# Low parts of the expert weights on VectorE, high parts a step ahead of them, X transposed beside the down products, loop over middle tiles behind the last tile

## The chip, the core and the metric

The kernel runs on one core of one Trainium2 chip. The metric is the device time of one execution in microseconds (us), as the median of several runs. The engines are named as the profile names them: PE is the matrix engine and PEld its loading of weights, DVE the vector engine, ACT the scalar engine, POOL or Pool is GpSimd, and SP is the engine whose queue issues most transfers. PEq, DVEq and so on stand for the sequencer of an engine.

## The reference

One decoder block over 1024 tokens of 1024 numbers, in float32. Two token mixers, a gated MLP over chunks and a windowed attention, come first, and neither is touched by the change. Behind them stands the mixture of experts, in which each token goes to two of 16 experts:

```python
def hierarchical_moe(h, rg_w, rg_b, re_w, re_b, w_gate, w_up, w_down):
    ...
    out = jnp.zeros_like(t)
    for e in range(N_EXPERTS):
        hid = jax.nn.silu(t @ w_gate[e]) * (t @ w_up[e])
        out = out + combine[:, e:e + 1] * (hid @ w_down[e])
    return out.reshape(B, S, D)
...
h = h + hierarchical_moe(hn, ...)
return rms_norm(h, final_norm_g)
```

## The kernel before

The projections, the mixers and the routing take the first 640 us or so. The routing writes each token's row into a queue in memory for each of its experts (`xs_d`). The expert stage then goes through the experts e = 0 to 15, one after the other, the last fourteen in an order by their number of tokens.

**Weights as granules.** The weights of an expert are 12 granules of 128 x 1024 numbers: eight of gate and up, in two transfers of 256 KB each, and four of down, in one of 512 KB. The transfers are issued in SP's queue and land in nine raw buffers. PE multiplies in a 32-bit format of fewer digits (`fp32r`), so each granule is split in two. The high part is a copy on ACT (line 292 with the scale of the norm for gate and up, line 297 for down). The low part is raw times scale minus high: on DVE for gate and up (line 295), and on Pool for the four granules named in `POOL_LO` (line 301), except for the last expert, whose four are on DVE. A matrix product is then three matmuls (lines 193 to 195): high x high, high x low, low x high. A raw buffer is free for its next load when the low part is done, and the split tile when PE has read it.

**One expert.** `expert_tile` computes a tile of 128 tokens. The gate and up products fill two PSUM banks, f = 0 and f = 1, in steps ("k", 0) to ("k", 3), then f = 0 to its end, then f = 1. `hidden(f)` is a silu on ACT (line 1361) and a product on DVE (line 1362). `hidden_T(f)` transposes the result on PE (line 1368) and splits it into `hT` (lines 170 and 171). Between hidden(0) and hidden_T(0) PE has only two steps, gate_up(1, 4) and gate_up(1, 5). Then come four down products (line 1406), with hidden_T(1) behind the first. The result is scaled into `yt`, one half on ACT (line 1423) and one on DVE (line 1424), and added to the rows of `h_d` by an indirect transfer that Pool issues (line 1429).

**Work ahead.** While the main tile of expert e runs, `ahead(step)` places the work for expert e + 1 between its steps: loads, splits of granules 3 to 11 as listed in `AHEAD` (`AHEAD_0` and `AHEAD_1` for e = 0 and 1), and the transposes of its tokens (`transpose_x`, line 1318). `split` issues the high part, the low part, and the load that takes the raw buffer next. All engines run their instructions in the order in which this code writes them, so an instruction that waits holds up all behind it on its engine.

**Last tiles.** In front of its main tile an expert with more than 128 tokens has a last tile (`more_tiles`). For a remainder of up to 64 it is a `half_tile` (names end in `h`: 2h, 4h, 6h, 8h, 10h in this data), else a full one (12l, 15l). With it the first two steps of the main tile are done, and granules 0 to 2 of the next expert are split: `fill(0)` and `fill(1)`. An expert of up to 128 tokens (the odd ones, and 14) does the two fills alone. Between the branch (line 1573) and the last tile stands a loop over middle tiles (lines 1574 and 1575), for experts with more than 256 tokens, which this data has none of: it is skipped.

The functions that the diff touches, and what calls them, with the line numbers of the profile:

Of the kernel before, what the change touches and what calls it, by code (L numbers as in the profile page):

```python
# [19 lines left out]
P = 128  # L20
# [28 lines left out]
FIRST = 3  # L49
AHEAD = {("k", 1): (3, 4), ("k", 2): (5,), ("f1", 5): (6, 7), ("f1", 7): (8,), ("y", 0): (9, 10), ("y", 1): (11,)}  # L50

AHEAD_0 = {("f1", 7): (3, 4), ("y", 0): (5, 6, 7), ("y", 1): (8, 9, 10, 11)}
AHEAD_1 = {("f1", 5): (3, 4, 5), ("f1", 7): (6,), ("y", 0): (7, 8, 9), ("y", 1): (10, 11)}
ORDER_AT = {("f1", 5), ("y", 2)}
# [6 lines left out]
BESIDE = {("k", 1), ("k", 2), ("k", 3), ("f1", 5), ("f1", 7), ("y", 0), ("y", 1)}  # L61

POOL_LO = (8, 9, 10, 11)

# [15 lines left out]
def kernel(  # L80
# [160 lines left out]
    class Granules:  # L241
# [41 lines left out]

        def fill(self, g, pool_lo=(), later=None):

            w, k = self.split_tiles[g], g % 12
            raw, hi, low = self.raw[g], w[:, 0, :], w[:, 1, :]
            if k < KT:  # L290
                f = g2T[:, k : k + 1]
                nc.scalar.activation(hi, raw, AF.Copy, scale=f)  # L292

                def lo():
                    nc.vector.scalar_tensor_tensor(low, raw, f, hi, ALU.mult, ALU.subtract)  # L295
            else:
                nc.scalar.activation(hi, raw, AF.Copy)  # L297
                eng = nc.gpsimd if k in pool_lo else nc.vector

                def lo():  # L300
                    eng.tensor_tensor(low, raw, hi, ALU.subtract)  # L301
            if later is None:
                lo()
            else:
                later.append(lo)

        def split(self, g, *args, **kw):

            while len(self.split_tiles) <= g:
                self.take(len(self.split_tiles))  # L310
            self.fill(g, *args, **kw)
            for more in LOAD_AFTER.get(g, (g + 9,)):
                self.load(more)

    granules = Granules()
    early = []
    lows = []
    region = ExitStack()
# [74 lines left out]
    with ExitStack() as dctx:  # L393
# [266 lines left out]
        def half(hf, xh, vln, first):  # L660
# [252 lines left out]
            for nh in range(2):  # L913
# [5 lines left out]
                for i in range(HT):  # L919
# [17 lines left out]
                    if last and i == HT - 1:  # L937
                        granules.split(7, later=lows)
                    routed = {i: i for i in range(HT)} if hf == 1 else {1: 0, 3: 2}
# [405 lines left out]
    def expert_tile(  # L1345
# [77 lines left out]
        nc.scalar.activation(yt[:, 0:512], ys[0], AF.Copy, scale=cw)  # L1423
        nc.vector.tensor_scalar(yt[:, 512:D], ys[1], cw, None, ALU.mult)
        if dup is not None:
# [115 lines left out]

    def hint_more(e, n):

        tc.mark_branch_hint_location(f"more{e}", hint=n > P, engines=[mybir.EngineType.PE])

    def more_tiles(e, n, xlast, mlast, fill, first):
# [25 lines left out]

        with tc.If(n > P, label=f"more{e}") as more:
            with tc.If(n > 2 * P):
                with tc.For_i(1, (n - 1) // P, 1) as j:
                    startm = nc.s_assert_within(
                        j * P + first_row(e), 0, NE * CAP - P,
                        skip_runtime_bounds_check_because="1 <= j < (n - 1) // P <= 7",
                    )
                    xm, mm = transpose_x(  # L1580
                        load_x(xs_d[bass.ds(startm, P), :], f"{e}m", "yt"), f"{e}m", xT=xT
                    )
                    expert_tile(xm, mm, e, None, f"{e}m", **banks)
            last_tile(f"{e}")
        with more.Else():
# [8 lines left out]
    xT, meta = transpose_x(xearly[0], "0", 2, xs_d[0:P, D:XW])  # L1594
    lows[0]()
    place_tables(slice(0, 2), ebase)
    xnext = first_rows(1)
    n, *lasts = last_rows(0)
    hint_more(0, n)
    for g in range(9, 15):  # L1600
        granules.split(g, POOL_LO)

    nc.scalar.activation(one, one, AF.Silu)
    ordering = order_experts()
    for e in range(NE - 1):
# [18 lines left out]
        def ahead(step):  # L1624
            if e == 0 and step in ORDER_AT:
                next(ordering)
            if step == ("k", 0):
                got["n"] = last_rows(e + 1)
            if step == ("f1", 5) and e + 2 < NE:
                hint_more(e + 1, got["n"][0])  # L1630
            if step == ("f1", 7):
                got["x"] = transpose_x(xnext, f"{e + 1}")
            for j in (AHEAD_0, AHEAD_1, AHEAD)[min(e, 2)].get(step, ()):
                if 12 * (e + 1) + j < 12 * NE:
                    granules.split(12 * (e + 1) + j, POOL_LO if e + 2 < NE else ())
            if step == ("y", 0) and e + 2 < NE:
                got["next"] = first_rows(e + 2)
# [231 lines left out]
```

## Time and profile before

| | |
|---|---|
| median of 3 runs | 1130.58 us (1128.57 to 1130.84) |
| the profiled execution | 1130.55 us, its span 1128.8 us |
| busy share of the span | PE 92%, DVE 64%, ACT 53%, POOL 25% |
| mean granted clock of PE | 0.965 |

The span runs from the first to the last instruction; 1.75 us lie around it. The busy shares are means over the whole span, the expert stage alone is what the change touches. Matmuls overlap, so their durations sum to more than the time they take. A row with "<-" at its end names what released the instruction from its wait.

### The profile page before, as it was taken

The page shows a single profiled execution, that of the slowest core. Times are in us where ns is not written, and L with a number is a line of the kernel's source. Part 1 is how long each engine was busy: PE and PEld are TensorE (multiplying, and loading weights), DVE is VectorE, ACT ScalarE, POOL GpSimd, SP SyncE. Part 2 cuts the span into 40 slices and gives each one's busy share as a digit, 9 for nine tenths or more (in the row PEclk, how much of TensorE's full clock was granted, in tenths as well). Part 3 has the DMA queues.
Part 4 walks back from the last instruction along what each step waited for, and adds up shares of the span by engine and source line. Part 5 has one row for each costly group of instructions (what it writes and reads, how often), then busy time and mean ns, then how long its engine had stood idle before and what let it go on. Part 6 is the DMA issues. An engine that isn't in the chain of part 4 may idle for free. (4 is left out here: it accounts for less than half of the span.)

```text
span 1128.8 us, 15722 instructions
## 1 busy us (share of the span) xinstructions
PE 1036.0 (92%) x4775; PEld 833.4 (74%) x4775; DVE 726.0 (64%) x1592; ACT 598.6 (53%) x1000; POOL 280.3 (25%) x196
## 2 busy tenths in 40 slices
PE   7999899999999999999999777899898989898973
PEld 6778788788888888877888655677676767686762
DVE  6852567664468546774465889676776666657754
ACT  4543456543456445553354355575756666647451
POOL 4001000000012000000000424554646464626433
PEclk9999899999999999999999888999999989999996
DMA  7433545653247223226473549798979897968763
GB/s 240 131 94 117 182 153 166 187 159 131 75 154 242 91 77 91 57 75 187 131 261 128 197 149 270 236 288 270 308 243 312 249 319 222 311 220 283 232 235 136
DMA packets 125502, 214.72 MB, mean 190 GB/s; under 512 B 11563, under 2 KB 58731, under 8 KB 125360
## 3 DMA queue, kind: packets, MB, share of 16 engines
q1 hardware_dynamic: 112016, 176.58, 48.3%
q0 software_dynamic: 7200, 21.20, 7.0%
q10 hardware_dynamic: 6144, 15.27, 3.7%
q8 instruction: 62, 1.02, 0.4%
q14 instruction: 80, 0.66, 0.2%
HBM read 185.46 MB, written 37.63 MB: 198 GB/s over the span
## 5 line engine op out<-in xcount | busy, mean ns | idle before, releaser
L295 DVE SCALAR_TENSOR_TENSOR w_e<-raw_e,g2T,w_e 128x1024 fp32r<-128x1024 f32 x127 | 193.3, 1572 | 12.4 <-ACT w_e L292 10.1
L301 POOL TENSOR_TENSOR w_e<-raw_e,w_e 128x1024 fp32r<-128x1024 f32 x59 | 152.0, 2609 | 55.7 <-ACT w_e L297 55.4
L292 ACT ACTIVATE w_e<-raw_e,g2T 128x1024 fp32r<-128x1024 f32 x127 | 138.2, 1143 | 15.7 <-DMA raw_e<-in_expert_w_up_dram 4.6
L1071 POOL COPY row<-ids 128x1 int32<-128x1 int32 x8 | 4.2, 523 | 439.5 <-DVE w_e L295 227.8
L193 PE MATMUL ps_gu<-w_e,xT 128*128 128x512 f32 x256 | 105.8, 413 | 6.8 <-ACT w_e L297 4.1
L195 PE MATMUL ps_gu<-w_e,xT 128*128 128x512 f32 x256 | 103.4, 404 | 0.0
L194 PE MATMUL ps_gu<-w_e,xT 128*128 128x512 f32 x256 | 102.8, 402 | 0.0
L1406 PE MATMUL ps_y<-w_e,hT 128*128 128x512 f32 x384 | 98.6, 406 | 0.8 <-DVE hT L171 0.8
L1406 PEld LDWEIGHTS ps_y<-w_e,hT 128*128 128x128 f32 x384 | 70.8, 192 | 16.4 <-DVE hT L171 1.4
L297 ACT ACTIVATE w_e<-raw_e 128x1024 fp32r<-128x1024 f32 x63 | 63.0, 1052 | 1.5 <-DMA raw_e<-in_expert_w_down_dram 1.4
L193 PEld LDWEIGHTS ps_gu<-w_e,xT 128*128 128x128 f32 x256 | 49.4, 193 | 18.9 <-issue 8.7
L195 PEld LDWEIGHTS ps_gu<-w_e,xT 128*128 128x128 f32 x256 | 49.6, 194 | 11.8
L194 PEld LDWEIGHTS ps_gu<-w_e,xT 128*128 128x128 f32 x256 | 49.6, 194 | 10.2
L195 PE MATMUL ps_o<-w_wo,ms 128*128 128x512 f32 x128 | 51.3, 402 | 0.0
L194 PE MATMUL ps_o<-w_wo,ms 128*128 128x512 f32 x128 | 51.2, 400 | 0.0
L193 PE MATMUL ps_o<-w_wo,ms 128*128 128x512 f32 x128 | 51.1, 400 | 0.0
L193 PE MATMUL ps_ga<-xh,w_ga 128*128 128x512 f32 x128 | 50.7, 396 | 0.0
L194 PE MATMUL ps_ga<-xh,w_ga 128*128 128x512 f32 x128 | 50.6, 396 | 0.0
L195 PE MATMUL ps_ga<-xh,w_ga 128*128 128x512 f32 x128 | 50.6, 396 | 0.0
L559 PE MATMUL ps_gv<-w_gv,xh 128*128 128x512 f32 x192 | 46.9, 397 | 4.0 <-ACT xh L170 2.6
L194 PE MATMUL ps_gb<-xh,w_gb 128*128 128x512 f32 x128 | 50.5, 395 | 0.0
L195 PE MATMUL ps_gb<-xh,w_gb 128*128 128x512 f32 x128 | 50.5, 395 | 0.0
(554 smaller groups left out, 2494.1 us busy)
## 6 DMA issues: line engine op xcount, KB each, us to landing
raw_e<-in_expert_w_gate_dram SPq DMA_DIRECT2D x127, 256.0 KB
raw_e<-in_expert_w_up_dram SPq DMA_DIRECT2D x127, 256.0 KB
raw_e<-in_expert_w_down_dram SPq DMA_DIRECT2D x63, 512.0 KB
xs_d<-zero ACTq DMA_DIRECT2D x16, 516.0 KB
raw_ga<-in_w_in_dram SPq DMA_DIRECT2D x16, 512.0 KB
raw_gb<-in_w_in_dram SPq DMA_DIRECT2D x16, 512.0 KB
raw_wo<-in_w_out_dram SPq DMA_DIRECT2D x16, 512.0 KB
xt<-xs_d SPq DMA_DIRECT2D x15, 516.0 KB
```

Source lines behind the costliest of these rows:

```text
L193: nc.tensor.matmul(acc, lhi, rhi, start=start, stop=False)
L194: nc.tensor.matmul(acc, lhi, rlo, start=False, stop=False)
L195: return nc.tensor.matmul(acc, llo, rhi, start=False, stop=stop)
L292: nc.scalar.activation(hi, raw, AF.Copy, scale=f)
L295: nc.vector.scalar_tensor_tensor(low, raw, f, hi, ALU.mult, ALU.subtract)
L297: nc.scalar.activation(hi, raw, AF.Copy)
L301: eng.tensor_tensor(low, raw, hi, ALU.subtract)
L559: nc.tensor.matmul(accs[i], xh[a][k // 4][:, k % 4, t], gs[j][:, b, k % 2, :], start=k + a + b == 0, stop=k == KT - 1 and b == 1,)
L1071: nc.gpsimd.tensor_copy(row[:, D + 4 : D + 5].bitcast(I32), ids[:, n + i : n + i + 1])
L1406: nc.tensor.matmul(ys[nh], hT[:, a, k, :], dn[k][:, b, nh * 512 : (nh + 1) * 512], start=k + i == 0, stop=k == FK - 1 and i == 2,)
```

## The change

- `POOL_LO` goes: all low parts are on DVE. Pool keeps the copies of `meta`, indices and the indirect transfers.
- `split` falls into `high`, `low` and `load_others`. `AHEAD` lists them apart ("h3" is the high part of granule 3, "l3" its low part and the load behind it) and spreads them over more steps; from h7 on a high part stands a step ahead of its low part. `AHEAD_0` and `AHEAD_1` keep the steps in which they split.
- The transposes of the next tokens move from ("f1", 7), ahead of the down products, to ("y", 1), between the second and the third.
- The second half of `yt` is made on ACT.
- The loop over middle tiles moves behind the last tile, and PE gets a hint for its branch there.

```diff
-AHEAD = {("k", 1): (3, 4), ("k", 2): (5,), ("f1", 5): (6, 7), ("f1", 7): (8,), ("y", 0): (9, 10), ("y", 1): (11,)}
...
+AHEAD = {
+    ("k", 1): "h3 l3", ("k", 2): "h4 l4", ("k", 3): "h5 l5", ("f0", 5): "h6 l6", ("f0", 7): "h7",
+    ("f1", 5): "l7 h8", ("f1", 7): "l8 h9", ("y", 0): "l9 h10", ("y", 1): "l10 h11", ("y", 2): "l11",
+}
...
-POOL_LO = (8, 9, 10, 11)
...
+        def high(self, g):
...
+            nc.scalar.activation(self.split_tiles[g][:, 0, :], self.raw[g], AF.Copy, **scale)
+
+        def low(self, g):
+
+            w, raw, k = self.split_tiles[g], self.raw[g], g % 12
+            if k < KT:
+                nc.vector.scalar_tensor_tensor(
+                    w[:, 1, :], raw, g2T[:, k : k + 1], w[:, 0, :], ALU.mult, ALU.subtract
+                )
+            else:
+                nc.vector.tensor_tensor(w[:, 1, :], raw, w[:, 0, :], ALU.subtract)
...
         nc.scalar.activation(yt[:, 0:512], ys[0], AF.Copy, scale=cw)
-        nc.vector.tensor_scalar(yt[:, 512:D], ys[1], cw, None, ALU.mult)
+        nc.scalar.activation(yt[:, 512:D], ys[1], AF.Copy, scale=cw)
...
         with tc.If(n > P, label=f"more{e}") as more:
-            with tc.If(n > 2 * P):
+            hint(f"mid{e}", n > 2 * P)
+            last_tile(f"{e}")
+            with tc.If(n > 2 * P, label=f"mid{e}"):
                 with tc.For_i(1, (n - 1) // P, 1) as j:
...
-            last_tile(f"{e}")
...
-            if step == ("f1", 7):
+            if step == ("y", 1):
                 got["x"] = transpose_x(xnext, f"{e + 1}")
-            for j in (AHEAD_0, AHEAD_1, AHEAD)[min(e, 2)].get(step, ()):
-                if 12 * (e + 1) + j < 12 * NE:
-                    granules.split(12 * (e + 1) + j, POOL_LO if e + 2 < NE else ())
+            for part in (AHEAD_0, AHEAD_1, AHEAD)[min(e, 2)].get(step, "").split():
+                g = 12 * (e + 1) + int(part[1:])
+                if part[0] == "h":
+                    granules.high(g)
+                else:
+                    granules.low(g)
+                    granules.load_others(g)
```

Lines move by two to five: the silu is line 1363 after the change, the product 1364, the hidden transposes 1370, the halves of `yt` 1425 and 1426, the high parts 293, the low parts 299 and 303, the branch 1575, the skip of the loop 1578.

DVE's order in expert 6's main tile, from the third granule of the next expert on, before (line 295 is a gate/up low part, 1362 the product, 1392 the tokens' weights):

```order
L295 SCALAR_TENSOR_TENSOR w_e_10621<-raw_e_10015,g2T,w_e_10621 128x1024
L295 SCALAR_TENSOR_TENSOR w_e_10637<-raw_e_10021,g2T,w_e_10637 128x1024
L295 SCALAR_TENSOR_TENSOR w_e_10649<-raw_e_10061,g2T,w_e_10649 128x1024
L1362 TENSOR_TENSOR hid_0_10673<-hid_0_10673,ps_gu_0_10120 128x256
L295 SCALAR_TENSOR_TENSOR w_e_10685<-raw_e_10080,g2T,w_e_10685 128x1024
L295 SCALAR_TENSOR_TENSOR w_e_10691<-raw_e_10086,g2T,w_e_10691 128x1024
L171 TENSOR_TENSOR hT_10590<-ps_hT_0_10697,hT_10590 128x256
L1362 TENSOR_TENSOR hid_1_10708<-hid_1_10708,ps_gu_1_10121 128x256
L1392 ISA parts,cw_10711<-meta_10042,own 128x4
L1392 ISA cw_10711 128x1
L171 TENSOR_TENSOR xT_10714<-ps_xT_0_10717,xT_10714 128x512
```

And after the change (299 is the gate/up low part, 303 the down low part, 1364 the product):

```order
L299 SCALAR_TENSOR_TENSOR w_e_10642<-raw_e_10015,g2T,w_e_10642 128x1024
L299 SCALAR_TENSOR_TENSOR w_e_10664<-raw_e_10039,g2T,w_e_10664 128x1024
L299 SCALAR_TENSOR_TENSOR w_e_10676<-raw_e_10062,g2T,w_e_10676 128x1024
L299 SCALAR_TENSOR_TENSOR w_e_10688<-raw_e_10081,g2T,w_e_10688 128x1024
L1364 TENSOR_TENSOR hid_0_10702<-hid_0_10702,ps_gu_0_10138 128x256
L299 SCALAR_TENSOR_TENSOR w_e_10700<-raw_e_10112,g2T,w_e_10700 128x1024
L175 TENSOR_TENSOR hT_10611<-ps_hT_0_10720,hT_10611 128x256
L1364 TENSOR_TENSOR hid_1_10731<-hid_1_10731,ps_gu_1_10139 128x256
L1394 ISA parts,cw_10734<-meta_10095,own 128x4
L1394 ISA cw_10734 128x1
L303 TENSOR_TENSOR w_e_10718<-raw_e_10124,w_e_10718 128x1024
L175 TENSOR_TENSOR hT_10611<-ps_hT_1_10751,hT_10611 128x256
```

Four low parts of this list now stand ahead of the first product, where three stood (three more, from the fill, are ahead in both), and the down low parts come in between the rest, the first ahead of the second hT.

ACT's order at the same place, before (292 is a high part, 1361 a silu, 170 the high copy of hT and xT):

```order
L292 ACTIVATE w_e_10621<-raw_e_10015,g2T 128x1024
L292 ACTIVATE w_e_10637<-raw_e_10021,g2T 128x1024
L292 ACTIVATE w_e_10649<-raw_e_10061,g2T 128x1024
L1361 ACTIVATE hid_0_10673<-ps_gu_0_10120 128x256
L292 ACTIVATE w_e_10685<-raw_e_10080,g2T 128x1024
L292 ACTIVATE w_e_10691<-raw_e_10086,g2T 128x1024
L170 ACTIVATE hT_10590<-ps_hT_0_10697 128x256
L1361 ACTIVATE hid_1_10708<-ps_gu_1_10121 128x256
L170 ACTIVATE xT_10714<-ps_xT_0_10717 128x512
```

And after the change (293 is a high part, 1363 a silu, 174 the copy):

```order
L293 ACTIVATE w_e_10642<-raw_e_10015,g2T 128x1024
L293 ACTIVATE w_e_10664<-raw_e_10039,g2T 128x1024
L293 ACTIVATE w_e_10676<-raw_e_10062,g2T 128x1024
L293 ACTIVATE w_e_10688<-raw_e_10081,g2T 128x1024
L293 ACTIVATE w_e_10700<-raw_e_10112,g2T 128x1024
L1363 ACTIVATE hid_0_10702<-ps_gu_0_10138 128x256
L293 ACTIVATE w_e_10718<-raw_e_10124 128x1024
L174 ACTIVATE hT_10611<-ps_hT_0_10720 128x256
L1363 ACTIVATE hid_1_10731<-ps_gu_1_10139 128x256
L293 ACTIVATE w_e_10741<-raw_e_10605 128x1024
```

Five high parts stand ahead of the first silu where three stood, and the copies of xT are no longer ahead of the second hT.

PE's order before expert 6's last tile, before the change: from the end of the main tile of the expert ahead (1406) through the branch (1573) and the skip (1574) to the loop's own start (1575):

```order
L1406 MATMUL ps_y_1_10065<-w_e_9424,hT_9917 128x512 x3
L1573 COMPARE_AND_BRANCH
L1574 COMPARE_AND_BRANCH
L1575 REGISTER_ALU x2
L1575 COMPARE_AND_BRANCH
```

The loop's rows are left out here. Behind it stand the transposes of the half tile (1466), where the skip leads:

```order
L1574 UNCONDITIONAL_BRANCH
L1561 REGISTER_ALU x2
L1561 COMPARE_AND_BRANCH
L1466 MATMUL ps_xT_6h<-ident,xt_6l 128x64 x8
L193 MATMUL ps_gu_0_10120<-w_e_9450,xT_10041 128x512
```

After the change the transposes (1468) come behind the branch of line 1575 at once:

```order
L1408 MATMUL ps_y_1_10068<-w_e_9439,hT_9935 128x512 x3
L1575 COMPARE_AND_BRANCH
L1546 REGISTER_ALU
L1872 BRANCH_PREFETCH_HINT
L1563 REGISTER_ALU x2
L1563 COMPARE_AND_BRANCH
L1468 MATMUL ps_xT_6h<-ident,xt_6l 128x64 x8
L197 MATMUL ps_gu_0_10138<-w_e_9465,xT_10094 128x512
```

The skip (1578) then stands behind the last tile, whose down products are the rows of line 1408, and leads past the loop's start (1579) to the next steps of the main tile:

```order
L1408 MATMUL ps_y_6l_10396<-w_e_10115,hT_6l 128x512 x3
L1563 UNCONDITIONAL_BRANCH
L1578 COMPARE_AND_BRANCH
L1579 REGISTER_ALU x2
L1579 COMPARE_AND_BRANCH
```

So PE runs one skip in either order, ahead of the last tile before and behind it now.

## Rows read from the trace of the kernel before

**Rows 1.** The page: busy time of PE, share of the span, instructions.

```profile
PE 1036.0 (92%) x4775; PEld 833.4 (74%) x4775; DVE 726.0 (64%) x1592; ACT 598.6 (53%) x1000; POOL 280.3 (25%) x196
```

**Rows 2.** PE's waits, 646 to 1090 us: total us, times, longest us.

```profile
PE ps_hT L1368 <- DVE hid L1362: 27.5, 9, 6.2
PE ps_hT_2h L1503 <- DVE hid_2h L1497: 2.1, 1, 2.1
PE ps_hT_6h L1503 <- DVE hid_6h L1497: 1.2, 1, 1.2
PE ps_hT_4h L1503 <- DVE hid_4h L1497: 1.1, 1, 1.1
PE ps_hT_8h L1503 <- DVE hid_8h L1497: 0.9, 1, 0.9
PE ps_xT_2h L1466 <- DVEq L1574: 1.4, 1, 1.4
PE ps_xT_12l L1318 <- DVEq L1574: 1.2, 1, 1.2
```

**Rows 3.** Timelines of Pool, DVE, PE, 790 to 812: start, us, instruction, idle before.

```profile
791.42 10.53 POOL L301 TENSOR_TENSOR w_e<-raw_e,w_e 128x1024 fp32r<-128x1024 f32 x4 [5.40 <-ACT w_e L297]
...
796.80 11.02 DVE L295 SCALAR_TENSOR_TENSOR w_e<-raw_e,g2T,w_e 128x1024 fp32r<-128x1024 f32 x6 [0.21 <-ACT w_e L292]
...
799.61 3.42 DVE L295 SCALAR_TENSOR_TENSOR w_e<-raw_e,g2T,w_e 128x1024 fp32r<-128x1024 f32 x1
...
802.96 1.27 DVE L295 SCALAR_TENSOR_TENSOR w_e<-raw_e,g2T,w_e 128x1024 fp32r<-128x1024 f32 x1
...
807.74 0.41 DVE L1362 TENSOR_TENSOR hid<-hid,ps_gu 128x256 f32<-128x256 f32 x1
...
808.20 0.44 PE L1368 MATMUL ps_hT<-ident,hid 128*128 128x128 f32 x2 [3.07 <-DVE hid L1362]
```

**Rows 4.** Groups of instructions, 646 to 1085: count, busy us, mean ns, idle before.

```profile
L295 DVE SCALAR_TENSOR_TENSOR w_e<-raw_e,g2T,w_e 128x1024 fp32r<-128x1024 f32 x120 | 184.4, 1589 | 11.9 <-ACT w_e L292 9.6 <-DMA raw_e<-in_expert_w_up_dram 1.3 <-POOL meta L1311 0.9
L301 POOL TENSOR_TENSOR w_e<-raw_e,w_e 128x1024 fp32r<-128x1024 f32 x59 | 152.0, 2609 | 55.7 <-ACT w_e L297 55.4 <-PE ps_hT L1368 0.3
L292 ACT ACTIVATE w_e<-raw_e,g2T 128x1024 fp32r<-128x1024 f32 x119 | 129.2, 1143 | 9.4 <-DMA raw_e<-in_expert_w_up_dram 4.4 <-issue 2.3 <-PE ps_gu L195 2.0
L1423 ACT ACTIVATE yt<-ps_y,cw 128x512 f32<-128x512 f32 x15 | 10.3, 684 | 4.4 <-ACT w_e L297 2.8 <-POOL w_e L301 0.8 <-DMA raw_e<-in_expert_w_gate_dram 0.8
L301 DVE TENSOR_TENSOR w_e<-raw_e,w_e 128x1024 fp32r<-128x1024 f32 x4 | 4.8, 1222 | 0.5 <-DMA xt_15l<-xs_d 0.3 <-ACT w_e L297 0.2
```

**Rows 5.** Timeline of DVE in expert 0's stage, 675 to 694 us.

```profile
686.19 2.43 DVE L1285 TENSOR_SCALAR dup<-cnt 128x14 f32<-128x14 f32 x1
688.66 0.17 DVE L1287 CAST up<-dup 128x14 int32<-128x14 f32 x1
```

**Rows 6.** Timelines of PE before and behind expert 2's last tile.

```profile
707.83 0.68 PE L1466 MATMUL ps_xT_2h<-ident,xt_2l 64*128 64x64 f32 x8 [1.39 <-DVEq L1574]
...
725.50 0.39 PE L193 MATMUL ps_gu<-w_e,xT 128*128 128x512 f32 x1
725.72 0.39 PE L194 MATMUL ps_gu<-w_e,xT 128*128 128x512 f32 x1
```

**Rows 7.** Windows: us, busy PE, PEld, DVE, ACT, POOL; PE's clock, DMA share, GB/s.

```profile
666.94:670.35 3.41, 3.41 (x13) 2.72 (x12) 2.84 (x10) 0.77 (x2) 0.00 (x0) 0.50 0.03 11
694.24:701.07 6.83, 5.85 (x19) 4.96 (x20) 6.18 (x11) 3.93 (x7) 0.00 (x0) 0.50 0.97 255
751.00:805.00 54.00, 49.49 (x231) 39.09 (x229) 37.37 (x56) 36.16 (x49) 29.13 (x14) 1.00 0.90 277
1030.00:1060.00 30.00, 23.75 (x106) 18.72 (x105) 24.89 (x32) 19.26 (x25) 14.04 (x6) 0.94 0.99 308
```

**Rows 8.** Lines 1573 and 1574, PE's branches: ns min/median/max, first and last start.

```profile
L1573 PEldq COMPARE_BRANCH  x15: 77/357/4184, 648.8 to 1038.8; - x15
...
L1574 PEldq COMPARE_BRANCH  x6: 234/338/345, 703.8 to 980.4; - x6
```

More of the change, by code (lines that the diff above doesn't have):

```diff
@@ L49 @@
 FIRST = 3
-AHEAD = {("k", 1): (3, 4), ("k", 2): (5,), ("f1", 5): (6, 7), ("f1", 7): (8,), ("y", 0): (9, 10), ("y", 1): (11,)}
-AHEAD_0 = {("f1", 7): (3, 4), ("y", 0): (5, 6, 7), ("y", 1): (8, 9, 10, 11)}
-AHEAD_1 = {("f1", 5): (3, 4, 5), ("f1", 7): (6,), ("y", 0): (7, 8, 9), ("y", 1): (10, 11)}
+AHEAD = {
+    ("k", 1): "h3 l3", ("k", 2): "h4 l4", ("k", 3): "h5 l5", ("f0", 5): "h6 l6", ("f0", 7): "h7",
+    ("f1", 5): "l7 h8", ("f1", 7): "l8 h9", ("y", 0): "l9 h10", ("y", 1): "l10 h11", ("y", 2): "l11",
+}
+AHEAD_0 = {("f1", 7): "h3 l3 h4 l4", ("y", 0): "h5 l5 h6 l6 h7 l7", ("y", 1): "h8 l8 h9 l9 h10 l10 h11 l11"}
+AHEAD_1 = {
+    ("f1", 5): "h3 l3 h4 l4 h5 l5", ("f1", 7): "h6 l6", ("y", 0): "h7 l7 h8 l8 h9 l9", ("y", 1): "h10 l10 h11 l11",
+}
 ORDER_AT = {("f1", 5), ("y", 2)}
@@ L282, in take, with fill, load_others, split @@
             self.split_tiles.append(w)
[L284 to L307, printed above, removed]
+        def high(self, g):
             while len(self.split_tiles) <= g:
                 self.take(len(self.split_tiles))
-            self.fill(g, *args, **kw)
+            scale = {"scale": g2T[:, g % 12 : g % 12 + 1]} if g % 12 < KT else {}
+            nc.scalar.activation(self.split_tiles[g][:, 0, :], self.raw[g], AF.Copy, **scale)
[7 more added lines that the diff above has]
+                nc.vector.tensor_tensor(w[:, 1, :], raw, w[:, 0, :], ALU.subtract)
+        def fill(self, g):
+            self.high(g)
+            self.low(g)
+        def load_others(self, g):
             for more in LOAD_AFTER.get(g, (g + 9,)):
                 self.load(more)
+        def split(self, g):
+            self.fill(g)
+            self.load_others(g)
     granules = Granules()
     early = []
-    lows = []
     region = ExitStack()
@@ L937, in half @@
                     if last and i == HT - 1:
-                        granules.split(7, later=lows)
+                        granules.high(7)
                     routed = {i: i for i in range(HT)} if hf == 1 else {1: 0, 3: 2}
@@ L1540, in half_tile, with hint @@
         )
-    def hint_more(e, n):
-        tc.mark_branch_hint_location(f"more{e}", hint=n > P, engines=[mybir.EngineType.PE])
+    def hint(label, stays):
+        tc.mark_branch_hint_location(label, hint=stays, engines=[mybir.EngineType.PE])
     def more_tiles(e, n, xlast, mlast, fill, first):
@@ L1594 @@
     xT, meta = transpose_x(xearly[0], "0", 2, xs_d[0:P, D:XW])
-    lows[0]()
+    granules.low(7)
+    granules.load_others(7)
     place_tables(slice(0, 2), ebase)
@@ L1598 @@
     n, *lasts = last_rows(0)
-    hint_more(0, n)
+    hint("more0", n > P)
     for g in range(9, 15):
-        granules.split(g, POOL_LO)
+        granules.split(g)
     nc.scalar.activation(one, one, AF.Silu)
@@ L1629, in ahead @@
             if step == ("f1", 5) and e + 2 < NE:
-                hint_more(e + 1, got["n"][0])
-            if step == ("f1", 7):
+                hint(f"more{e + 1}", got["n"][0] > P)
+            if step == ("y", 1):
                 got["x"] = transpose_x(xnext, f"{e + 1}")
-            for j in (AHEAD_0, AHEAD_1, AHEAD)[min(e, 2)].get(step, ()):
-                if 12 * (e + 1) + j < 12 * NE:
-                    granules.split(12 * (e + 1) + j, POOL_LO if e + 2 < NE else ())
+            for part in (AHEAD_0, AHEAD_1, AHEAD)[min(e, 2)].get(step, "").split():
[5 more added lines that the diff above has]
+                    granules.load_others(g)
             if step == ("y", 0) and e + 2 < NE:
```

## The prediction

> **What bounds the kernel now.** I read the busy table first: PE works for 92% of the span [rows 1], so time can only come from PE's pauses, from its clock, or from work that is taken off it, and the change takes none off. I then asked what PE waits for in the expert stage, from 646 us on [rows 2]. Three kinds of wait stand there that the change touches. The transposes of the hidden tile (line 1368) wait for DVE's product of line 1362 nine times, 27.5 us in all, the longest 6.2. The transposes of a last tile wait at the branch of line 1574: 1.4 us in each of five half tiles (one row of the five is shown; in one of them another releaser is named) and 1.2 in expert 12, 8.2 in all. The half tiles' hidden transposes wait for DVE four times: 2.1 + 1.2 + 1.1 + 0.9 = 5.3.
>
> Why is the product late? In expert 5's stage [rows 3] Pool makes four low parts of the down weights in 10.53 us. Beside them one low part takes 3.42 us on DVE; the first one behind Pool takes 1.27. DVE runs its low parts and the product in program order, six low parts take 11.02 us, and the product comes at 807.74 with PE idle for 3.07. Over the stage the groups say the same [rows 4]: DVE's gate/up low part is 1589 ns in the mean, and a low part of a down granule is 2609 on Pool and 1222 on DVE, where the last expert has them. In expert 0's stage even DVE's 14-element table operations are held up: 2.43 us for one beside Pool, 0.17 for the like of it behind Pool [rows 5]. That is the 6.2.
>
> Last, PE's granted clock is half its full level behind some of these waits, in five stretches, three of 3.41 us and two of 6.83 (one of each is shown) [rows 7]: 23.9 us at 1.2 GHz, which at 2.4 would have taken half, so 11.9 us.
>
> **The change part by part.** The sum is made against the profiled execution's own 1130.55 us (span 1128.8); the median of the three runs, 1130.58, is the same.
>
> 1. *Low parts leave Pool.* 59 instructions of 2609 ns go, and 59 of 1222 come on DVE: 72 us more for DVE. Against it stand DVE's 120 gate/up low parts, which by the undisturbed 1.27 lose 0.32 each, 38 us, and 15 halves of the output row, which go to ACT at about 0.69 each [rows 4]. DVE is off the path except where PE waits for the product. There: six low parts took 11.02; now seven stand before the product, 7 x 1.22 = 8.5, so 2.5 earlier. The first low part comes about 0.6 later, since its high part on ACT stands behind the second half of the output row. The product is 1.9 earlier, and 3.07 becomes about 1.2. I put 1.2 for each of the nine waits: 27.5 - 9 x 1.2 = **+16.7**. Bounds: 0.6 left (first low part not late) and 1.8 (DVE, whose last down low part now ends behind PE's last product, starts another 0.6 late).
>
> 2. *Half tiles.* Their three low parts of the next expert ran beside Pool; without it the 5.3 goes: **+5.3**.
>
> 3. *High parts a step ahead.* The eighth high part (h7) now stands before the silu in ACT's queue. In some experts its slot is that of a granule read by PE just six matmuls before the hidden transposes, and then the silu starts up to 1.14 later [rows 4]. So experts with a last tile, six of them, which had no wait at their main tile, get one: h7 1.14, a silu of about the product's length (an estimate), the product 0.41 [rows 3] and their semaphores, against six matmuls as cover, which start every 0.22 [rows 6] (1.3): 0.6 to 1.6. I take 1.1: **-6.6**.
>
> 4. *Loop behind the last tile.* Now the loop is skipped between the main tile and the last tile, PE stands until DVE's output row is through, and its first transpose comes 1.39 late [rows 6]. In the changed order of instructions nothing of that kind stands before the last tile: **+8.2**. But the skip now stands behind it, where PE ran on with no pause (725.50, no idle time) [rows 6]. PE must drain, jump, and read a count anew. No row shows that price: below it is 0 if it hides, above it is the 1.4 of the present skip. The branch itself takes 0.34 [rows 8] and a drain about a matmul, 0.4; I take 0.9, six times: **-5.4**. ACT and DVE skip there too, but have slack in the half tile.
>
> 5. *X transposes beside the down products.* PE's work is the same, eight transposes. They no longer cover the second product: only down(0), six matmuls or 1.3 us, lies between. Silu plus product is 0.8, so nothing is lost as long as no high or low part squeezes in: 0. If one low part does, 1.2 per expert; that is in rival A.
>
> 6. *The second half of the output row on ACT.* ACT has the room; its price was put in step 1.
>
> 7. *Clock.* The waits of up to 1.4 us in this trace were not followed by half clock; those that were are among the longer. With the waits at 1.2 most of the 11.9 should return, but 15 new small ones come: I take **+9**, bounds 3.4 and 11.9.
>
> 8. *Transfers.* From 1030 to 1060 the DMA engines are busy for 0.99 of the time [rows 7]. There experts 13 and 14 run on what arrives, so I take back two waits of 1.2: **-2.4**. Before, over a pair of experts (751 to 805), the share is 0.90, so some 5 of 54 us are to spare, of which the forecast takes about 3.
>
> Sum: 16.7 + 5.3 - 6.6 + 8.2 - 5.4 + 9 - 2.4 = 24.8, so 1130.55 - 24.8 = **1106**. With each unknown at its two ends, and not all at once, the likeliest case lies in 1097 to 1116.
>
> **The rivals.**
>
> A. *The wait moves.* DVE's queue is now longer by two low parts per expert net, and PE pauses at the hidden transposes of every expert. If it stays at 2.0 in the nine (9.5 won) and 2.0 in the six (12 lost), the drain costs the full 1.4 (8.4 lost), and only the clock behind the longest wait comes back (3.4), the gain is 9.5 + 5.3 + 8.2 - 12 - 8.4 + 3.4 = 6: **1124**. For it: steps 3 and 4 each put a new wait where PE had none. Against it: 1.27 behind Pool. Chance 0.17.
>
> B. *Transfers set the pace.* Five pairs of experts each lose half of their 3 us, 7.5 in all, because the spare 5 us don't lie where the loads are late: **1113**. For it the 0.99 at the end of the stage, where this has come about; against it the 0.90 before [rows 7]. Chance 0.12.
>
> C. *Each new jump fetches code.* The branch of line 1573 took 4.18 us once, while the median is 0.36 [rows 8]. If the skip behind the last tile takes that six times instead of 0.9, 19.7 are lost: 1106 + 19.7 = **1126**; with the clock's 9 gone as well, **1135**. Against it: the skip of the same loop took at most 0.345 in all six experts. The Trainium skill, "Runtime: NRT & Kernel Launch", section on the instruction fetch mechanics, says that a taken branch whose target lies outside the window that is loaded waits for a fetch by DMA; by that rule all six could pay, since the skipped loop holds a whole tile's instructions. The trace has such a price once in 15, and none at this loop. Chance 0.06.
>
> D. *DVE becomes the bound (slower).* If the low parts stay slow without Pool, at the 1.59 of their mean, seven of them in 15 experts are each 0.37 later than I reckon: 38.9 us, or **1145**. It decides from 24.8 / (15 x 7) = 0.24 on, so from 1.46 per low part. For it: DVE gets all of the splitting. Against it: 1.27 while ACT, PE and a transfer by Pool all ran. Chance 0.05.
>
> E. *No effect*, since what hid the Pool work hides DVE's as well: nothing for it, as PE waits for DVE by name. 0.03.
>
> **How the numbers follow.** The forecast has 0.57, A 0.17, B 0.12, C 0.06, D 0.05, E 0.03. A change within 0.2% (2.3 us) can hardly be told from none here. The forecast, A and B are faster, as is half of C: 0.87 (A's edge takes a little); same 0.05; slower 0.08. The range, 1094 to 1124, takes in the forecast's own range, B, and half of A, and leaves out the far end of A, C, D and the best case, in which nearly all unknowns fall well (1087 at the least).
>
> **What would show it.** Low parts of 1.2 to 1.3 us throughout (step 1). The wait of PE for the product: about 1.2 in odd experts, in place of 3. No wait of last-tile transposes, and a new one of about 0.9 before the first matmul behind a last tile (step 4). In experts with a last tile a wait of about 1.1 for the product, with h7 on ACT just before the silu (step 3). No half clock between 660 and 1060. It would be wrong if PE waits for high parts whose raw data has just landed (B), if the pause behind the last tile is near 4 (C), or if PE's waits for the product come to over 25 us in the sum.

## The result and the profile after

The changed kernel takes 1124.75 us in the median of seven runs (1121.35 to 1126.08), the kernel before 1130.58 (1127.54 to 1131.93). The ratio is 0.9949 with an interval of 0.9932 to 0.9966: faster by 0.5%, 5.8 us, where I forecast 24.6. The time is that of rival A, which I gave 0.17. The profiled execution has a span of 1124.4 us.

PE's waits from 646 to 1090 us in the kernel after (total us, times, longest us), which answer to [rows 2]:

```profile
PE ps_hT L1370 <- DVE hid L1364: 20.4, 10, 4.7
PE ps_gu L197 <- PEq L1578: 11.2, 6, 2.4
...
PE ps_gu L197 <- DVE st L1283: 4.2, 1, 4.2
```

The half tiles' waits for the product and all but one of the waits in front of last tiles (0.8 is left in expert 2) are gone: 13.5 us together, less that 0.8. But PE still waits 20.4 for the product, where it waited 27.5, and 11.2 behind the last tiles, where it waited for nothing. The 4.2 for line 1283 stands at the start of expert 1, where the kernel before had a pause of 1.2; the wait of 6.2 for expert 1's product, 12 us later, is gone.

The groups of low parts after (count, busy us, mean ns, idle before), which answer to [rows 4]:

```profile
L299 DVE SCALAR_TENSOR_TENSOR w_e<-raw_e,g2T,w_e 128x1024 fp32r<-128x1024 f32 x120 | 147.2, 1280 | 22.8 <-ACT w_e L293 18.7 <-DMA raw_e<-in_expert_w_up_dram 1.7 <-issue 1.5
L303 DVE TENSOR_TENSOR w_e<-raw_e,w_e 128x1024 fp32r<-128x1024 f32 x63 | 75.1, 1218 | 0.8 <-ACT w_e L293 0.8
```

So the durations of step 1 came out, 1280 and 1218 ns, and yet PE waits. Timelines of ACT, DVE and PE in expert 7 (start, us, instruction, idle before) show on what:

```profile
847.96 7.39 ACT L293 ACTIVATE w_e<-raw_e,g2T 128x1024 fp32r<-128x1024 f32 x7
857.93 1.15 ACT L293 ACTIVATE w_e<-raw_e,g2T 128x1024 fp32r<-128x1024 f32 x1 [2.58 <-DMA raw_e<-in_expert_w_up_dram]
858.98 0.37 ACT L1363 ACTIVATE hid<-ps_gu 128x256 f32<-128x256 f32 x1
...
859.38 0.42 DVE L1364 TENSOR_TENSOR hid<-hid,ps_gu 128x256 f32<-128x256 f32 x1 [1.73 <-ACT hid L1363]
...
859.86 0.69 PE L1370 MATMUL ps_hT<-ident,hid 128*128 128x128 f32 x2 [2.80 <-DVE hid L1364]
```

The row at 857.93 is h7. ACT stands 2.58 us for its raw granule, the silu stands behind it in the queue, and PE 2.80 behind both. The wait is put down to DVE, as in [rows 2]. There DVE was late; here DVE itself stands idle for 1.73 until the silu is done. The same goes for experts 9, 11 and 14: in these four PE waits 2.2 to 4.7, 13.7 of the 20.4 us. The other six waits are 0.5 to 1.4.

The half clock came back as it was. Windows of the five stretches between 660 and 1060 (columns as in [rows 7]):

```profile
681.90:688.73 6.83, 5.66 (x13) 4.47 (x14) 6.21 (x20) 0.76 (x1) 1.30 (x1) 0.50 1.05 351
722.86:726.27 3.41, 3.19 (x8) 2.55 (x9) 2.48 (x2) 1.98 (x3) 2.16 (x2) 0.50 0.68 213
859.40:862.81 3.41, 2.95 (x8) 2.47 (x9) 2.02 (x3) 1.28 (x2) 0.00 (x0) 0.50 1.06 326
972.04:975.45 3.41, 3.41 (x9) 2.64 (x9) 1.91 (x6) 1.33 (x2) 0.00 (x0) 0.50 1.06 207
1050.54:1057.37 6.83, 4.03 (x11) 3.25 (x12) 3.06 (x5) 3.49 (x6) 0.74 (x1) 0.50 0.85 285
```

Again 23.9 us in the sum. Each begins in or right behind a pause of PE of 2.3 us or more: the first in the pause at the start of expert 1, the second behind expert 2's half tile, where there was no pause before, and the last three, 13.7 us together, at the waits for h7 in experts 7, 11 and 14.

### The profile page after: what moved, and what is told of

Read it like the earlier page. It is cut to its first block, busy times and chain, and to the rows that moved or that the text cites. A ratio compares the mean times of both kernels' runs of the same rounds, so it can differ in the third digit from the quotient of the medians.

```text
span 1124.4 us, 15697 instructions
## 1 busy us (share of the span) xinstructions
PE 1035.1 (92%) x4775; PEld 829.4 (74%) x4775; DVE 730.6 (65%) x1635; ACT 606.7 (54%) x1016; POOL 118.2 (11%) x137
## 5 line engine op out<-in xcount | busy, mean ns | idle before, releaser
L299 DVE SCALAR_TENSOR_TENSOR w_e<-raw_e,g2T,w_e 128x1024 fp32r<-128x1024 f32 x127 | 156.2, 1280 | 23.4 <-ACT w_e L293 19.2
L197 PE MATMUL ps_gu<-w_e,xT 128*128 128x512 f32 x256 | 107.6, 420 | 20.0 <-PEq L1578 11.2
L1408 PE MATMUL ps_y<-w_e,hT 128*128 128x512 f32 x384 | 101.4, 407 | 1.4 <-ACT hT L174 0.9
L303 DVE TENSOR_TENSOR w_e<-raw_e,w_e 128x1024 fp32r<-128x1024 f32 x63 | 75.1, 1218 | 0.8 <-ACT w_e L293 0.8
L293 ACT ACTIVATE w_e<-raw_e 128x1024 fp32r<-128x1024 f32 x63 | 65.8, 1056 | 4.2 <-PE ps_gu L199 4.1
L199 PE MATMUL ps_gb<-xh,w_gb 128*128 128x512 f32 x128 | 50.5, 395 | 0.0
L198 PE MATMUL ps_gb<-xh,w_gb 128*128 128x512 f32 x128 | 50.5, 395 | 0.0
L197 PE MATMUL ps_gb<-xh,w_gb 128*128 128x512 f32 x128 | 50.5, 395 | 0.0
```

Of the source, the lines that this page charges most:

```text
L197: nc.tensor.matmul(acc, lhi, rhi, start=start, stop=False)
L198: nc.tensor.matmul(acc, lhi, rlo, start=False, stop=False)
L199: return nc.tensor.matmul(acc, llo, rhi, start=False, stop=stop)
L293: nc.scalar.activation(self.split_tiles[g][:, 0, :], self.raw[g], AF.Copy, **scale)
L299: nc.vector.scalar_tensor_tensor(w[:, 1, :], raw, g2T[:, k : k + 1], w[:, 0, :], ALU.mult, ALU.subtract)
L303: nc.vector.tensor_tensor(w[:, 1, :], raw, w[:, 0, :], ALU.subtract)
```

## The experiments

Ratios are to the kernel before, run beside it on the same chip; the changed kernel's is 0.9949. Differences in us are between medians, unless a ratio is named; by the ratios they come out up to 2.6 us otherwise. Runs are named by their number: x7 is x7_lows_only.

**Which part gave and which took: the change's parts alone.** The first is the kernel before with one edit:

```diff
-POOL_LO = (8, 9, 10, 11)
+POOL_LO = ()
```

> The kernel before (1129.8 us) with its down low parts on DVE and nothing else changed, in the old order. Theory P (Pool beside DVE makes the product late): gate/up low parts of 1.28 us, the waits of 27.5 us for the product fall below 15, 1114 to 1120 us. Theory N (the order matters as much: the down low parts now stand in DVE's queue ahead of hT, the output row and the next granules): 1124 to 1132 us.

Measured: 1113.17 us, 0.9860 (0.9844 to 0.9877). Theory P holds, below its range, and this edit alone gains three times what the whole change does. The three largest of the six waits in front of last tiles in this run:

```profile
PE ps_xT_2h L1466 <- DVEq L1574: 4.3, 1, 4.3
...
PE ps_xT_12l L1318 <- DVEq L1574: 3.0, 1, 3.0
...
PE ps_xT_6h L1466 <- DVEq L1574: 2.1, 1, 2.1
```

Of the 27.5 us of waiting for the product in nine places nothing is left (I had left 1.2 in each). What grows is the skip in front of the last tiles, 15.3 in six for 8.2, since DVE's half of the output row now stands behind its low parts. DVE's timeline in expert 5, beside [rows 3]:

```profile
792.30 7.27 DVE L295 SCALAR_TENSOR_TENSOR w_e<-raw_e,g2T,w_e 128x1024 fp32r<-128x1024 f32 x6
799.48 0.41 DVE L1362 TENSOR_TENSOR hid<-hid,ps_gu 128x256 f32<-128x256 f32 x1
```

Six low parts take 7.27 for 11.02, and the product stands right behind them.

Four kernels then put one other part of the change on top of this one. The loop behind the last tile, with the hint:

```diff
-            with tc.If(n > 2 * P):
+            tc.mark_branch_hint_location(f"mid{e}", hint=n > 2 * P, engines=[mybir.EngineType.PE])
+            last_tile(f"{e}")
+            with tc.If(n > 2 * P, label=f"mid{e}"):
...
-            last_tile(f"{e}")
```

> x7_lows_only (1113.2 us) with the loop over middle tiles behind the last tile and its hint, as the change has it. In x7 the skip in front costs 15.3 us in six waits. Theory F (behind the half tile the branch fetches code): five pauses near 2 and one of 0.8 take their place, about 11, with more half clock behind them: 1109 to 1116 us, little won. Rival (the move is worth what I forecast, 8.2 against 5.4, and more here): 1103 to 1107 us.

Measured: 1117.1 us, 0.9879 (0.9865 to 0.9893), a little above theory F's range: the pauses behind the last tiles are 10.9 us in six for 15.3 in front, but PE now waits elsewhere for 5.4 (2.0 for expert 2's half tile's X, 1.8 and 1.6 for X rows that have not landed).

The output row's second half on ACT:

```diff
-        nc.vector.tensor_scalar(yt[:, 512:D], ys[1], cw, None, ALU.mult)
+        nc.scalar.activation(yt[:, 512:D], ys[1], AF.Copy, scale=cw)
```

> x7_lows_only with the second half of the output row on ACT. Theory Y (DVE's output row is what the skip in front of a last tile waits for): the waits there fall from 15.3 to about 9: 1106 to 1110 us. Rival (ACT's next high part comes 0.7 later, and with it the first low part and the product): 1112 to 1117 us.

Measured: 1109.43 us, 0.9804 (0.9783 to 0.9824), in theory Y's range, though the waits in front of last tiles fall only to 12.2 from 15.3, where about 9 were expected.

The X transposes between the down products:

```diff
-            if step == ("f1", 7):
+            if step == ("y", 1):
                 got["x"] = transpose_x(xnext, f"{e + 1}")
```

> x7_lows_only with the transposes of the next X between the second and third down products. Theory X (they were the cover of the second product): hidden_T(1) or its copy comes late by 0.4 to 1 us in each of 15 experts: 1118 to 1127 us. Rival (down(0) is cover enough, as I forecast): 1111 to 1115 us.

Measured: 1122.93 us, 0.9939 (0.9917 to 0.9961). Theory X. PE now waits for the low copy of hT in every one of 15 experts (before the edit three times):

```profile
PE ps_y L1406 <- DVE hT L171: 5.0, 15, 0.5
```

That is 0.33 each, 3.4 more than without the edit (1.6); the skip in front costs 1.8 more, and half clock (3.41 us each time) follows all six of these pauses, where it followed three.

The new lists, `high` and `low` apart, all else as in the first of these kernels (this is the changed kernel with its three other parts undone):

```diff
-        nc.scalar.activation(yt[:, 512:D], ys[1], AF.Copy, scale=cw)
+        nc.vector.tensor_scalar(yt[:, 512:D], ys[1], cw, None, ALU.mult)
...
-            hint(f"mid{e}", n > 2 * P)
-            last_tile(f"{e}")
-            with tc.If(n > 2 * P, label=f"mid{e}"):
+            with tc.If(n > 2 * P):
...
+            last_tile(f"{e}")
...
-            if step == ("y", 1):
+            if step == ("f1", 7):
                 got["x"] = transpose_x(xnext, f"{e + 1}")
```

> x7_lows_only with the new lists: high parts a step ahead, seven low parts ahead of the product instead of six, h7 ahead of the silu; loop, output row and X transposes as before. Theory Q (that order is what eats the gain of the lows): waits for the product of 1 to 4 us come back in most experts, 15 to 20 us in all: 1123 to 1130 us. Rival (the order is harmless, the loop or X is what costs): 1111 to 1116 us.

Measured: 1122.34 us, 0.9919 (0.9902 to 0.9935), just below theory Q's range and far from the rival's. The waits for the product are back, but smaller than theory Q had them, 12.2 in 13 places and none over 1.4:

```profile
PE ps_hT L1370 <- DVE hid L1364: 12.2, 13, 1.4
```

In six of them (1.3 to 1.4 each, 7.9 in all) the silu is late behind h7; in the other seven (0.4 to 0.8 each, 4.3 in all) the product stands behind a low part. No h7 here waits for its transfer; in the six it waits for PE, which still reads its slot.

On the low parts' 0.9860 the loop adds 0.0019, the output row takes 0.0056, X adds 0.0079 and the order 0.0059: 0.9961 in the sum, and the changed kernel has 0.9949. The sum comes near, but its interval is about 0.006 either way, and the parts do not simply add: what X costs alone is not found in the changed kernel (x17 below), and h7 waits for transfers there, which it does not here.

**The same parts undone in the changed kernel.** h7 behind the silu:

```diff
-    ("k", 1): "h3 l3", ("k", 2): "h4 l4", ("k", 3): "h5 l5", ("f0", 5): "h6 l6", ("f0", 7): "h7",
-    ("f1", 5): "l7 h8", ...
+    ("k", 1): "h3 l3", ("k", 2): "h4 l4", ("k", 3): "h5 l5", ("f0", 5): "h6 l6",
+    ("f1", 5): "h7 l7 h8", ...
```

> The changed kernel (1124.75 us) with h7 behind the first silu instead of ahead of it. Theory Q (order on ACT): PE's waits of 2.8, 2.2, 4.0 and 4.7 us for the product in experts 7, 9, 11 and 14 come from h7 standing ahead of the silu while its raw granule has not landed; behind the silu they fall to about 1 each, so 9 us fewer waits, some half clock back: 1113 to 1117 us. Theory T (transfers set the pace): granule 7 still lands when it lands, and the wait reappears at hT or at the next silu: 1122 to 1126 us.

Measured: 1118.2 us, 0.9905 (0.9887 to 0.9923), between the two theories: the waits for the product fall from 20.4 to 8.9, but all five pauses behind half tiles are now followed by 3.41 us of half clock, where one was.

The loop in front of the last tile again, without hint, as in the diff of the lists above:

> The changed kernel with the loop over middle tiles in front of the last tile again, and no hint for it. Theory S (each skip costs PE a drain, wherever it stands): the 11.2 us behind the last tiles go, about 1.4 us in front of each of six last tiles come back (8.2 in the kernel before), so 1120 to 1123 us. Theory T (transfers set the pace): 1123 to 1126 us, the waits go to the product.

Measured: 1128.1 us, 0.9985 (0.9968 to 1.0001), slower than both theories. In this order the place behind was worth 3.4 us. The skip in front costs as much as the one behind did, 11.4 in six, 4.0 of it in expert 2.

No loop at all:

```diff
-            hint(f"mid{e}", n > 2 * P)
             last_tile(f"{e}")
-            with tc.If(n > 2 * P, label=f"mid{e}"):
...
```

> The changed kernel without the loop over middle tiles, which this data never enters (it would leave out the middle tiles of an expert with more than 256 tokens). Theory S: the 11.2 us go and nothing comes: 1112 to 1116 us. Theory T: PE gets to the product earlier, and waits longer there for what has not landed: 1120 to 1125 us.

Measured: 1108.56 us, 0.9812 (0.9796 to 0.9827): 16.2 less than the changed kernel, more than theory S's 11.2. Theory T falls with it: from experts 4 and 5 to 10 and 11 a pair goes through in 51 to 54 us (from end to end of its last down products), where the changed kernel takes 54 to 57, so the transfers could follow. The 5 us beyond the 11.2 show in the clock: from 660 us to the last matmul half clock lasts 17.1 us here and 30.7 in the changed kernel, and PE's busy time for the same matmuls is 396.1 us for 400.9.

The down low parts on Pool, in the new order:

```diff
-                nc.vector.tensor_tensor(w[:, 1, :], raw, w[:, 0, :], ALU.subtract)
+                eng = nc.gpsimd if g < 12 * (NE - 1) else nc.vector
+                eng.tensor_tensor(w[:, 1, :], raw, w[:, 0, :], ALU.subtract)
```

> The changed kernel with the low parts of the down granules on Pool again (the last expert's stay on DVE), in the changed order. Theory P (Pool's low parts beside DVE's were the cost): gate/up low parts back near 1.6 us in the mean, waits for the product up by 8 to 17 us: 1132 to 1142 us. Theory N (moving them was worth little, since DVE got 72 us for the 38 it won): 1123 to 1128 us.

Measured: 1130.66 us, 0.9998 (0.9982 to 1.0014), between the theories, and neither's mechanism. Pool's low parts overlap with DVE's gate/up low parts for 14 us in this order, where it was 55 in the kernel before; DVE's are 1308 ns in the mean:

```profile
L299 DVE SCALAR_TENSOR_TENSOR w_e<-raw_e,g2T,w_e 128x1024 fp32r<-128x1024 f32 x120 | 150.7, 1308 | 30.3 <-ACT w_e L293 26.1 <-DMA raw_e<-in_expert_w_gate_dram 2.1 <-DMA raw_e<-in_expert_w_up_dram 1.1
```

The X transposes at their old place:

```diff
-            if step == ("y", 1):
+            if step == ("f1", 7):
                 got["x"] = transpose_x(xnext, f"{e + 1}")
```

> The changed kernel with only the X transposes back at their old place, ahead of the down products. Theory X (they cover the second product, and the five units of waiting at hT in x12_lows_xT are theirs): 6 to 9 us faster, 1116 to 1119 us. Rival (in the new order hT is early enough, and the waits are h7's and the skip's): 1122 to 1125 us.

Measured: 1122.49 us, 0.9937 (0.9914 to 0.996), in the rival's range. The interval takes in the changed kernel's 0.9949: what costs 9 us alone can't be told from nothing here. PE's waits for the low copy of hT, 5.0 us in x12, are 0.5 in the changed kernel, so there was little to win back.

**What the skip costs behind a half tile.** The profile after has it in PE's branches at line 1578 (columns as in [rows 8]; two for each last tile, the skip and a second one of 0.2 us):

```profile
L1578 PEldq COMPARE_BRANCH  x12: 191/276/3371, 718.9 to 1002.1; - x12
```

Five of the twelve take 2.6 to 3.4 us, all behind half tiles; behind the full tile of expert 12 the same branch takes 0.35 and the pause is 0.8. In each of the five, and in none of the other seven, a transfer of 16 KB begins in queue q8, which the page lists as one of instructions. Between 718.9 and 722.3 us, the time of the first (queue, transfers, MB, share):

```profile
q8 instruction: 1, 0.02, 2.3%
```

First the hint, given behind the branch between half and full tile instead of ahead of it:

```diff
-            hint(f"mid{e}", n > 2 * P)
             last_tile(f"{e}")
...
             with tc.If((n - 1) % P < H) as few:
+                hint(f"mid{e}", n > 2 * P)
...
             with few.Else():
+                hint(f"mid{e}", n > 2 * P)
```

> The changed kernel (1124.75 us) with PE's hint for the skip given behind the branch between half and full tile, in each of the two, instead of ahead of it. Theory F (code fetch): the five branches of 2.6 to 3.4 us behind the half tiles become 0.2 to 0.4, PE's pause there falls from 11.2 us in six to about 5 (0.8 each, a drain), and the half clock behind it goes: 1114 to 1119 us. Theory S (the drain itself, whatever the branch takes): pauses as they are, 1123 to 1126 us.

Measured: 1122.27 us, 0.9929 (0.9916 to 0.9943), between the theories. The five long branches are still there (2.6 to 3.6 us) and the pauses 11.6: as a remedy it does nothing, and it tells nothing of the cause.

Together with h7 behind the silu, as in x1_h7_late:

> x1_h7_late and x5_hint_late together. If the two causes are separate, the two gains add up (6.5 and 6 to 10): 1108 to 1113 us. If transfers set the pace underneath, the second gain turns into waits for raw granules: 1115 to 1118 us.

Measured: 1117.52 us, 0.9887 (0.9871 to 0.9902), x1_h7_late again, since the hint gave nothing. The range is that of the second case, but with no second gain to lose the run says nothing on transfers.

Then the half tile's code was put next to the skip, by turning the branch round:

```diff
-            with tc.If((n - 1) % P < H) as few:
-                half_tile(xlast, xT, mlast, e, f"{name}h", fill)
-            with few.Else():
+            with tc.If((n - 1) % P >= H) as few:
...
+            with few.Else():
+                half_tile(xlast, xT, mlast, e, f"{name}h", fill)
```

> The changed kernel (1124.75 us) with the two branches of the last tile in the other order in the program: the full tile's code first, the half tile's behind it, right ahead of the skip. Theory F (the branch fetches code when the half tile's end has jumped over the full tile's code): the five branches behind half tiles fall from 2.6 to 3.4 us to 0.4 and the pauses there from about 2 to 0.8, as behind the full tile of expert 12, whose own pause grows; but the jump over the full tile's code now stands ahead of the half tile and may fetch there. 1116 to 1122 us if it does not, 1122 to 1127 if it does. Theory S (a drain costs 2 whatever the code): pauses stay near 2 without any long branch, 1123 to 1126 us.

Measured: 1125.72 us, 0.9964 (0.9946 to 0.9982). The branches of line 1578 and PE's largest waits in this run:

```profile
L1578 PEldq COMPARE_BRANCH  x12: 194/264/384, 717.3 to 997.6; - x12
```

```profile
PE ps_hT L1370 <- DVE hid L1364: 22.8, 10, 5.2
PE ps_gu L197 <- PEq L1578: 4.9, 6, 0.8
```

No branch of this line is long any more, no transfer of q8 begins in one, and the pauses are 0.8 each, 4.9 in six: theory F is shown, the pause without a fetch is 0.8 and the fetch the rest. Nor is there a fetch at the jump that now stands ahead of the half tile: its branch (line 1563) takes 0.35 to 0.38. But the median is that of the changed kernel. Of the 6.3 us that PE no longer pauses there, 2.4 are now in the wait for the product (22.8) and 1.4 in a wait of the last expert (1.8 for 0.4); half clock from 660 us to the last matmul is 30.7 us in both. The rest is not accounted for, as the profiled executions lie apart: this one is the fastest of nine, that of the changed kernel the slowest of seven. If the wait for the product is h7 ahead of the silu, moving h7 as in x1_h7_late must give both gains:

> x14_half_near (skip without a fetch, 1125.7 us) with h7 behind the first silu, as in x1_h7_late. Theory H (h7 ahead of the silu turned the won 6 us into waits for its raw granule: 22.8 us of waiting for the product there): those waits fall below 10 and both gains show, 1108 to 1114 us. Theory T (the transfers as a whole are late, wherever h7 stands): 1117 to 1124 us.

Measured: 1112.28 us, 0.9832 (0.9815 to 0.9849): theory H. The waits for the product are 8.4, 14.4 less than in x14. But more than half of that comes back at the next place, as h8 is now ahead of hT on ACT:

```profile
PE ps_y L1408 <- ACT hT L174: 8.8, 7, 2.3
PE ps_hT L1370 <- DVE hid L1364: 8.4, 7, 2.8
```

So long waits became short ones, and much of the gain is clock: half clock from 660 us to the last matmul is 17.1 us, where x14 has 30.7, and PE's busy time for the same matmuls 397.3 us for 401.6.

**The pause of 4.2 us at the start of expert 1.** In expert 0's stage DVE makes four down low parts at ("y", 1), ahead of the counts and tables (lines 1269 and 1283) that PE's sequencer waits for. Behind the tables, on top of x6_both:

```diff
-... ("y", 1): "h8 l8 h9 l9 h10 l10 h11 l11"}
+... ("y", 1): "h8 h9 h10 h11", ("y", 2): "l8 l9 l10 l11"}
```

> x6_both with the four down low parts of expert 0's stage behind the table operations in DVE's order instead of ahead of them. Theory R (the 4.2 us that PE stands before expert 1 are those low parts, ahead of the counts that PE's sequencer reads): 3 to 4.2 us off x6_both, and 1.7 to 3.4 more where the half clock behind that pause goes. Rival: the low parts come late for expert 1 instead, and the time stays that of x6_both within 1.5 us.

Measured: 1114.65 us, 0.986 (0.9845 to 0.9875), 2.9 less than x6_both, with the 4.2 gone: just below theory R's lower end. But the rival has its part in it: PE now waits 3.3 for expert 1's product, where it did not, and the half clock at this place is 3.41 us for 6.83.

**The best of the parts.** Low parts on DVE and the output row on ACT in the old order (x11), first without a loop (middle tiles are left out, of which there are none), as a bound:

> x11_lows_yt (1109.4 us) without the loop over middle tiles (which this data never enters). The skip in front costs x11 12.2 us in six waits. If nothing else stands there: 1095 to 1100 us. If DVE or the transfers are as late: 1102 to 1107 us. It bounds what any place of the loop can give.

Measured: 1092.45 us, 0.9649 (0.9628 to 0.967), below my range: 17 us for a skip whose waits sum to 12.2. Here, too, the rest shows in the clock: half clock from 660 us to the last matmul is 17.1 us, where x11 has 27.3, and PE's busy time is 396.6 us for 401.6. Then with the loop behind the last tile and the half tile next to it (the diffs of x9 and x14):

> x11_lows_yt with the loop behind the last tile and the half tile's code next to the skip. Theory F without a fetch ahead: six pauses of 0.8 in place of 12.2 us: 1100 to 1105 us. With a fetch on one side or the other: 1108 to 1114 us.

Measured: 1101.97 us, 0.9737 (0.9718 to 0.9756), in the range of theory F without a fetch ahead. And with the tables ahead of the last splits of expert 0's stage:

```diff
-ORDER_AT = {("f1", 5), ("y", 2)}
+ORDER_AT = {("f1", 5), ("y", 1)}
```

> x16_best_near (1102.0 us) with expert 0's table operations one step earlier in the program, ahead of its last four splits on DVE. The 4.4 us before expert 1 go: 1096 to 1100 us. If the low parts are then late for expert 1: 1100 to 1103 us.

Measured: 1098.22 us, 0.9714 (0.9695 to 0.9733), in the first range. The 4.4 is gone, and again a wait for expert 1's product stands in its place, 3.6, with less half clock behind it. This kernel is faster than the changed one by 26 us and than the kernel before by 33; it has three parts of the change (low parts, output row, loop) and not the other two, and two edits that the change has not (the half tile's place, the tables).

## Why the prediction was wrong

Steps 3, 4 and 7 failed. In numbers, of the 19 us between the forecast and the measured gain, 9 stand in step 7, 5.8 in step 4, and 3.0 in the pause at the start of expert 1 (4.2 for 1.2), which no step had; the rest are small terms of both signs. The steps one by one:

1. *Low parts leave Pool, +16.7.* Right for the edit: 17.0 us alone (x7), by the mechanism named, 1.28 us per low part. In the changed kernel the nine waits, put at 1.2 each and 10.8 in all, come to 16.3, because of step 3.
2. *Half tiles, +5.3.* Right.
3. *High parts a step ahead, -6.6.* The mechanism of this step failed. I let h7 cost its own 1.14 us, and only in experts with a last tile; there it is near, 1.3 to 1.4 in three of the six, 4.1 in all. What the profile after shows besides is that h7 waits for its transfer with the silu behind it, in experts 7, 9, 11 and 14: 2.58 us in expert 7, and ACT's waits of this kind come to 13.0 (2.9 of them for h6). It is the case that I named as the sign of B, but the transfers as a whole were not the pace: x3 and x15 go through faster. h7's place is worth 6.5 us in the changed kernel (x1) and 13.4 with the skip's fetch gone (x18 against x14). That the waits for the product sum to 20.4, where steps 1, 3 and 8 had left 10.8 + 6.6 + 2.4 = 19.8, is luck: I had many waits near 1.1, and half clock follows three of the four long ones.
4. *Loop behind the last tile, +8.2 and -5.4.* The first is right but for the 0.8 left in expert 2. The other term was mis-sized by half: 11.2. Its cause is rival C's, to which I gave 0.06: a fetch at five of six skips. I took the 0.34 of the present skip [rows 8] as the price, though there PE comes straight from the code ahead of it, and behind a half tile it has just jumped over a full tile's code. Nor did line 1573 pay such a price once in 15, as I read from its greatest value: it took 4.18, 3.66 and 3.92 us, at 649, 738 and 1039. The Trainium skill, "Runtime: NRT & Kernel Launch", section on the instruction fetch mechanics, says that a taken branch to code that is not loaded waits for a fetch by DMA. The rows agree: with a transfer of q8 in it the skip takes 2.6 to 3.4, without one, in x14, 0.38 at the most.
5. *X transposes, 0.* Wrong alone, 9 us (x12): down(0) is not cover enough by 0.33 us, and half clock follows more of the skip's pauses. In the changed kernel it can't be told from 0 (x17).
6. *Output row on ACT, 0.* A gain of 0.0056 alone, some 6 us by the ratios and 3.7 by the medians (x11); part of it is that the skip in front no longer waits for DVE's half of the row. In the changed kernel, whose skip stands elsewhere, this was not measured.
7. *Clock, +9.* Nothing: 23.9 us at half clock before and after. I let the gain follow from waits of 1.2, but the pauses that are left or new are of 2 to 4.7, at h7 (step 3), behind half tiles (step 4) and at the start of expert 1.
8. *Transfers, -2.4.* Experts 13 and 14 still wait, 1.0 and 4.7; the 4.7 is step 3's.

So the reading of the bound was right, and the sum was wrong because the parts' costs were taken from rows in which the cover still stood. Rival A had the time and the form (the wait moves). Its prices are not what happened: it had 30 us of waiting for the product for 20.4, 8.4 behind the last tiles for 11.2, and 3.4 back from the clock for nothing, so that its sum came out is in good part luck.

## What to carry to other kernels

Where one edit of several carries the gain, price the others by asking what each takes away as cover: the transposes that were moved cost 9 us alone, though PE's work was the same. Ahead of an instruction that the busiest engine waits for, put nothing that depends on a transfer: h7 behind the silu was worth 6.5 and 13.4 us. Do not look at the sum of the waits alone: at the two places that x18's edit touches PE waits 17.2 us for 23.7 in x14, in shorter pieces, and the time falls by twice that difference, much of it by the clock. And price a branch by the code that it jumps over and from where, not by a like branch elsewhere.

## What was not expected of the hardware

The skip's branch on PE took 0.2 to 0.4 us, or 2.6 to 3.4 in the profile after where it came right behind a jump over a tile's code, with a 16 KB transfer of instructions in each of these; moving the hint changed nothing (x5), moving the code did (x14). It is not so every time: in expert 10 of x9 and x17 the same branch took 0.25. A pause of PE of 2 us or more was often, not always, followed by half clock, five times of nine between 660 and 1085 us of the profile after, and then for 3.41 or 6.83 us; so a pause of 2 can cost near 4 (an estimate: half of 3.41 on top). And the slowing of DVE's low parts beside Pool, 1.59 us in the mean, depends on the order: with as many low parts on Pool in the new order it was 1.31 (x4).
